# The moving operand of every weight product read by turns from two halves of its columns, and one group of seven products fewer in eight

## The chip, the cores and the metric

The kernel runs on one core of a Trainium2 chip. The metric is the time on the device in microseconds (us), the median over runs. The engines have their usual names: TensorE (PE in the profile; its weight loads are PEld), VectorE (DVE), ScalarE (ACT), GpSimd (POOL) and SyncE (SP, which here only issues DMAs).

## What is computed

One layer of a decoder in float32, 256 tokens, model width 2048: a SwiGLU feed-forward, a mixer of two kinds of attention, a second feed-forward. The weight products are nearly all of the work.

```python
h = x + 0.5 * swiglu(rms_norm(x, g1), w_gate1, w_up1, w_down1)      # 2048 -> 5632 -> 2048
u = rms_norm(h, gm)
proj = u @ w_in        # q, k, v and forget logits of 16 forgetting heads; q, k, v of 16 + 4 + 4 windowed heads
o = concat(rms_norm(forgetting_attention), rms_norm(sliding_window_sink_attention))
h = h + o @ w_out
y = h + 0.5 * swiglu(rms_norm(h, g2), w_gate2, w_up2, w_down2)
# swiglu(x, wg, wu, wd) = (silu(x @ wg) * (x @ wu)) @ wd
```

## The kernel before

**A product.** Each float32 weight and each activation is split into a high part, rounded to the matmul's input format (fp32r), and a low part, the rest. `mm3` multiplies a 128x128 stationary block of activations with 512 columns of weights (the moving operand) as three matmuls: high by high, high by low, low by high. The three stand on lines 400, 401 and 402, whoever calls `mm3`. In the mixer one projection has blocks of 388 columns. Only these products take weights; transposes, scores and the sums over values are plain fp32 matmuls on other lines (602 turns a feed-forward's rows, 1320 makes scores).

**Making the parts.** SyncE loads a weight tile (`raw`, 128x2048 in a feed-forward), ScalarE casts it (`whi`), VectorE subtracts (`wlo`, line 464). One of four subtractions in most down parts is on GpSimd (line 466, `BESIDE`).

**Groups.** A tile of a feed-forward's up part holds four blocks of 512 columns: two rows of blocks (k) of the gate's weights and two of the up weights. With two tiles of tokens that is a 2x2 by 2x2 product of blocks. A group of kind D does it with the plain eight products. A group of kind S does it with seven, in Winograd's form: four of the seven take sums of weight blocks, which VectorE makes (line 531 the outer two, line 538 the inner two), ScalarE casts and VectorE splits again (line 464, `sums`). Sums of activations (`fu`) are made once for each pair of k (`form_of`), and VectorE combines the results at the end of a unit (line 733).

**Units.** A feed-forward goes over 11 blocks of 512 hidden columns. A unit ("U") is one block: eight groups, whose kinds the table `UNITS` gives; a down part ("D") takes the block's result through the down weights in four groups of kind D. `PLAN` has units and down parts by turns. In between stand transposes (line 602).

**What sets the order.** For each feed-forward `arrange` plays the tasks through with costs and due times that the code gives (a product 0.681, `cast`, `sub`, `slow` for GpSimd's subtraction) and limited buffers, and the order that comes out of it is each engine's order in the program. TensorE's own order of products is that of `main`, with the transposes put in between. In the mixer the order comes from the framework's scheduler.

Of the kernel before, what the change touches and what calls it, by code (L numbers as in the profile page):

```python
# [18 lines left out]
D = 2048  # L19
# [11 lines left out]
SWC = NSW // 4  # L31
# [3 lines left out]
    mybir.EngineType.PE, mybir.EngineType.DVE, mybir.EngineType.Activation, mybir.EngineType.Pool, mybir.EngineType.SP  # L35
}
NB = FF // 512
UNITS = [["D" * 8, x, "DSSSSSSD"] + ["SSSSSSSD"] * (NB - 3) for x in ("DDSSDSSD", "DSSDSSSD")]
DOWN = "DDDD"
BESIDE = (1,)  # L40
AT_Q2 = True
# [1 line left out]
PLAN = [("U", 0)] + [x for b in range(1, NB) for x in (("U", b), ("D", (b - 1,)))][:-1] + [("D", (NB - 2, NB - 1))]  # L43
NRAW = 4
NSUM = 2
NHI = 5
NLO = 5
SCRATCH = 512
FREE2 = 2
F2_ORDER = [(0, "rawy", F32)] + [(2, "whiy", F32R), (3, "wloy", F32R)] * FREE2 + [(1, "sums", F32)] * NSUM  # L50
F2_ORDER += [(2, "whiy", F32R)] * (NHI - 2 - FREE2) + [(3, "wloy", F32R)] * (NLO - 2 - FREE2) + [(0, "rawy", F32)] * (NRAW - 3)
PAD = 48
# [47 lines left out]


def slow(n):
    return 0.4 + 0.0021 * n


class Task:
# [167 lines left out]
def hybrid_layer(ctx: ExitStack, tc: tile.TileContext, a: dict, out: bass.AP):  # L274
# [69 lines left out]
    def mean_rsqrt(pool, ssq, n, width, tag):  # L344

        own = "rm" if pool is sp else tag
        x = pool.tile([P, n], F32, tag=own + "x", name=tag + "x")
        y = pool.tile([P, n], F32, tag=tag + "y", name=tag + "y")
        t = pool.tile([P, n], F32, tag=own + "t", name=tag + "t")
        nc.vector.tensor_scalar(  # L350
            out=x, in0=ssq, scalar1=1.0 / width, scalar2=EPS, op0=ALU.mult, op1=ALU.add
        )
        nc.vector.tensor_scalar(
            out=t.bitcast(I32), in0=x.bitcast(I32), scalar1=1, scalar2=None,
            op0=ALU.logical_shift_right,
        )
        nc.vector.tensor_scalar(
            out=y.bitcast(I32), in0=t.bitcast(I32), scalar1=-1.0, scalar2=float(0x5F3759DF),
            op0=ALU.mult, op1=ALU.add,
        )  # L360
        for _ in range(3):
            nc.vector.tensor_tensor(out=t, in0=y, in1=y, op=ALU.mult)
            nc.vector.scalar_tensor_tensor(
                out=t, in0=t, scalar=-0.5, in1=x, op0=ALU.mult, op1=ALU.mult
            )
            nc.vector.scalar_tensor_tensor(
                out=y, in0=t, scalar=1.5, in1=y, op0=ALU.add, op1=ALU.mult
            )
        return y
# [18 lines left out]
    def rstd_tokens(ssq, width, tag):  # L388
# [7 lines left out]
                )  # L396
        return mean_rsqrt(sp, pb[:, :NT], NT, width, tag)

    def mm3(o, shi, slo, mhi, mlo, start, stop, seeded=False):
        nc.tensor.matmul(o, lhsT=shi, rhs=mhi, start=start, stop=False, skip_group_check=seeded)  # L400
        nc.tensor.matmul(o, lhsT=shi, rhs=mlo, start=False, stop=False, skip_group_check=seeded)  # L401
        return nc.tensor.matmul(o, lhsT=slo, rhs=mhi, start=False, stop=stop, skip_group_check=seeded)  # L402
# [29 lines left out]
    def ffn(pool, u, wgu, wd, slots, banks, rstd, held=None, first=None, lead=None, done=None, out=None):  # L432
# [10 lines left out]
        def task(*args, **kw):  # L443
            t = Task(*args, **kw)
            tasks.append(t)
            return t
# [12 lines left out]
        def bank_of(b):  # L459
            return banks[b["first"].got["bank"][0]]  # L460
# [84 lines left out]

        def product(held, key, stat, w, need):

            t = task("pe", 0.681, None, list(need) + w[0], lag=0.25)
            b = held.setdefault(key, {"first": t})
            if "seed" in b and "last" not in b:  # L550
                t.need.append(b["first"])
            if b["first"] is t:
                t.take = {"bank": 1}
            b["last"] = t

            def run():
                t.made = mm3(bank_of(b), *stat(), *w[1](), start=b["first"] is t, stop=b["last"] is t, seeded="seed" in b)

            t.run = run
            main.append(t)  # L560
            return t
# [89 lines left out]
        forms = {}  # L651
        units = UNITS[0 if first is not None else 1]
        count, seven_of = [k.count("S") for k in units], PAIRS[0 if first is not None else 1]
# [195 lines left out]
                        later.append(c)  # L849

        if lead is not None:
            proj = task("pe", 10.8, None, give=[(k, list(ids)) for k, ids in held.items() if k != "bank"])
            main.append(proj)
            res = [task("dve", 0.75, lambda t=t: lead["residual"](t), [proj], 12, give=[("bank", [t])], psum=True) for t in range(NT)]
            un, ssq, gcol = lead["next"]
            lead_squares = squares_of(ssq, 3, [[r] for r in res], 50)
            turned(lambda: h[:, :, 3 * 512 :], 3, res, into_u(un, gcol, 45))
# [44 lines left out]
    def more_slots(pool):  # L902

        return [
            [pool.tile([P, 2048], dt, name="%s%d" % (nm, i)) for i in range(n)]
            for nm, dt, n in (("rawx", F32, NRAW - 2), ("sums", F32, NSUM), ("whix", F32R, NHI - 2), ("wlox", F32R, NLO - 2))
        ]

    def join(slots, own_first):

        raws, sums, his, los = slots
        return [
            (x + r if own_first else r + x) for r, x in ((rings[0], raws), ([], sums), (rings[1], his), (rings[2], los))
        ]
# [66 lines left out]
    with tc.tile_pool(name="mix", bufs=1) as mp:  # L981
# [197 lines left out]
        for t in range(NT):  # L1179
            for aa in range(2):  # L1180
                n = nqk // 2
# [211 lines left out]
    with tc.tile_pool(name="f2", bufs=1, reuse_waits=REUSE) as fp:  # L1393
        slots = [[], [], [], []]
        for i, nm, dt in F2_ORDER:
# [3 lines left out]
            fp, u2, a["wgu2"], a["wd2"], join(slots, True), acc, lambda: rstd_blocks(ss2, "rm"),  # L1399
            {"hi": range(FREE2, NHI), "lo": range(FREE2, NLO), "bank": (0, 1)},  # L1400
            lead={"residual": last_quarter, "next": (u2, ss2, V_G2)}, out=out.rearrange("(t p) d -> p t d", p=P),
# [4 lines left out]
def _arrays(x, positions, norm_ffn1_g, ffn1_w_gate, ffn1_w_up, ffn1_w_down, norm_mix_g, w_in, b_forget,  # L1406
            fox_q_norm_g, fox_k_norm_g, swa_q_norm_g, swa_k_norm_g, swa_sinks, out_norm_fox_g, out_norm_swa_g,
            w_out, norm_ffn2_g, ffn2_w_gate, ffn2_w_up, ffn2_w_down):
    f32 = np.float32
    d = {}  # L1410

    def blocks(w, rows, cols):

        n, m = w.shape
        w = w.reshape(n // P // rows, rows, P, m // cols, cols).transpose(3, 0, 2, 1, 4)
        return w.reshape(m // cols, n // P // rows, P, rows * cols)

    def cols(w):
        return blocks(w, 2, 512)

    def twos(w0, w1):

        x = np.stack([cols(w0).reshape(-1, w0.shape[0] // (2 * P), P, 2, 512), cols(w1).reshape(-1, w1.shape[0] // (2 * P), P, 2, 512)])
        x = np.stack([x[0, ..., 0, :], x[0, ..., 1, :], x[1, ..., 1, :], x[1, ..., 0, :]], -2)
        return x.reshape(*x.shape[:-2], 2048)

    def by_two(w):
        v = w.reshape(w.shape[0], -1, 2, 512)
        return twos(v[:, :, 0].reshape(w.shape[0], -1), v[:, :, 1].reshape(w.shape[0], -1))

    d["wgu1"], d["wd1"] = twos(ffn1_w_gate[0], ffn1_w_up[0]), by_two(ffn1_w_down[0])
    d["wgu2"], d["wd2"] = twos(ffn2_w_gate[0], ffn2_w_up[0]), by_two(ffn2_w_down[0])
    w = w_in[0]
    nf = NH * HD
    d["ws"] = blocks(w[:, 3 * nf :], 2, SWC)
    d["wf"] = np.stack([blocks(w[:, i * nf : (i + 1) * nf], 2, 512) for i in range(3)], 1)
    d["wo"] = np.stack([cols(w_out[0][:nf]), cols(w_out[0][nf:])])
    d["xT"] = x[0].T.reshape(KD // 2, 2, P, SEQ).transpose(0, 2, 1, 3)
    d["x"] = x[0].reshape(NT, P, D)
    d["pos"] = positions[0].reshape(NT, P).T  # L1440

    vec = np.zeros((P, V_END), f32)
    for col, g in (
        (V_G1, norm_ffn1_g), (V_GM, norm_mix_g), (V_G2, norm_ffn2_g), (V_GF, out_norm_fox_g), (V_GS, out_norm_swa_g),
    ):
        n = g.shape[1] // P
        vec[:, col : col + n] = g[0].reshape(n, P).T
    vec[:, V_BF : V_BF + NH] = b_forget[0]
    vec[:, V_SINK : V_SINK + NH] = swa_sinks[0]
    vec[:, V_SQ : V_SQ + HD] = swa_q_norm_g[0]  # L1450
    vec[:, V_SK : V_SK + HD] = swa_k_norm_g[0]
    vec[:HD, V_FQ] = fox_q_norm_g[0]
    vec[:HD, V_FK] = fox_k_norm_g[0]
    vec[HD : HD + 2, V_FQ : V_FK + 1] = 1.0
    d["vec"] = vec

    cst = np.zeros((P, C_END), f32)
    i, j = np.arange(P)[:, None], np.arange(P)[None, :]
    cst[:, C_ID : C_ID + P] = i == j
    cst[:, C_ONE : C_ONE + P] = 1.0  # L1460
    cst[:, C_TRI : C_TRI + P] = i <= j
    cst[:, C_MSK : C_MSK + P] = np.where(j > i, 0.0, NEG)
    for m in (C_MSK + P, C_MSK + 3 * P):
        cst[:, m : m + P] = np.where(j <= i, 0.0, NEG)
    cst[:, C_INVF : C_INVF + 32] = (10000.0 ** (-np.arange(0, HD, 2, dtype=np.float64) / HD)).astype(f32)
    d["cst"] = cst
    return {k: np.ascontiguousarray(v) for k, v in d.items()}
# [17 lines left out]
```

## Time and profile before

| what | value |
|---|---|
| median of 3 runs | 1734.43 us (1733.5 to 1734.45) |
| the profiled execution's own time | 1734.49 us |
| its span, first to last instruction | 1732.7 us |
| TensorE busy, matmuls | 1721.5 us (99%), 7989 |
| VectorE busy | 1557.7 us (90%) |
| ScalarE busy | 1161.1 us (67%) |
| GpSimd busy | 106.7 us (6%) |
| moved by DMA | 339.73 MB, mean 196 GB/s |

The stages lie so in the span: first feed-forward to about 650 us, mixer to about 1050 us, second feed-forward to the end. A matmul's busy time is modelled (its end is not recorded), and matmuls overlap each other; how fast TensorE goes is therefore read from the distance of starts. "wlo<-raw,whi" means that the instruction writes `wlo` and reads `raw` and `whi`. An "x8" behind a row of the timeline says that eight instructions were merged in it. A row of waits ends in total us, times and longest.

### The profile page before, as it was taken

Reading aid. Unit: us, or ns where it says so; the run is one execution under the profiler, and the core shown is the slowest. Engines: PE = TensorE matmul, PEld = TensorE weight load, DVE = VectorE, ACT = ScalarE, POOL = GpSimd, SP = SyncE. Lnnn points to the kernel's source line nnn. Section 1 sums busy time; section 2 is a strip of 40 time slices with the busy share of each in tenths; the row PEclk is TensorE's granted clock in tenths of the full one; section 3 lists DMA queues with packets and bytes.
Section 4 is the critical chain, followed back from the end, with each engine's and each line's share of the span. In section 5 each row is a group of like instructions: output and inputs, shape, how many; then the busy total and the mean of one; then the engine's idle time right before and its main releaser. Section 6 shows DMA issues by size and latency. Waiting matters only on the chain.

```text
span 1732.7 us, 21114 instructions
## 1 busy us (share of the span) xinstructions
PE 1721.5 (99%) x7989; PEld 1431.7 (83%) x7989; DVE 1557.7 (90%) x1724; ACT 1161.1 (67%) x1416; POOL 106.7 (6%) x40
## 2 busy tenths in 40 slices
PE   9999999999999999999999999999999999999999
PEld 6888888888888888998788888888888888888887
DVE  7999999999999996668777769999999999999994
ACT  6677777767776764555766556667767777776761
POOL 0011001101101100000000000001101101100100
PEclk9999999999999999999999999999999999999999
DMA  9556456556645653574444456446556646655652
GB/s 366 196 215 219 168 202 240 204 182 216 223 172 217 219 205 128 168 212 153 137 145 145 134 202 259 166 174 224 196 189 218 242 160 223 220 186 194 232 194 97
DMA packets 62918, 339.73 MB, mean 196 GB/s; under 512 B 6752, under 2 KB 15456, under 8 KB 29280
## 3 DMA queue, kind: packets, MB, share of 16 engines
q1 hardware_dynamic: 62208, 337.18, 54.8%
q8 instruction: 62, 1.02, 0.2%
q0 software_dynamic: 320, 1.05, 0.1%
q14 instruction: 40, 0.33, 0.1%
q10 hardware_dynamic: 288, 0.16, 0.0%
HBM read 336.27 MB, written 2.10 MB: 195 GB/s over the span
## 4 chain that ended last, share of the span: by engine, by line
PE 97%; DVE 1%; DMA 1%; ACT 1%; SPq 0%; issue 0%; DVEq 0%; ACTq 0%
PE acc L401 25%; PE acc L400 25%; PE acc L402 25%; PE sm L401 6%; PE sm L402 6%; PE sm L400 6%; PE acc L602 1%; PE sm L1131 1%; PE sc L1320 1%; DMA rawx<-in_wgu 1%; PE sm L1137 1%; PE sm L602 0%; PE sm L1299 0%; DVE wloy L464 0%; PE sc L1245 0%; PE sm L1138 0%
## 5 line engine op out<-in xcount | busy, mean ns | idle before, releaser
L400 PE MATMUL acc<-whi,u 128*128 128x512 f32 (+1 forms) x659 | 251.5, 383 | 1.1 <-DVE s L1095 0.9
L401 PE MATMUL acc<-wlo,u 128*128 128x512 f32 (+1 forms) x659 | 251.2, 382 | 0.8 <-DVE wlo L464 0.8
L402 PE MATMUL acc<-whi,u 128*128 128x512 f32 (+1 forms) x659 | 249.9, 381 | 0.0
L317 DVE TENSOR_TENSOR wlo<-raw,whi 128x1024 fp32r<-128x1024 f32 (+1 forms) x112 | 128.8, 1154 | 74.0 <-ACT whi L316 73.5
L316 ACT CAST whi<-raw 128x1024 fp32r<-128x1024 f32 (+1 forms) x112 | 111.0, 991 | 96.3 <-PE acc L402 87.0
L400 PEld LDWEIGHTS acc<-whi,u 128*128 128x128 f32 x659 | 123.7, 188 | 23.5 <-DVE s L1095 1.3
L401 PEld LDWEIGHTS acc<-wlo,u 128*128 128x128 f32 x659 | 123.7, 188 | 21.7 <-DVE wlo L464 1.1
L402 PEld LDWEIGHTS acc<-whi,u 128*128 128x128 f32 x659 | 123.6, 188 | 21.1 <-issue 0.8
L464 DVE TENSOR_TENSOR wlo<-sums,whi 128x2048 fp32r<-128x2048 f32 x53 | 121.2, 2287 | 3.2 <-ACT whi L519 2.3
L464 DVE TENSOR_TENSOR wlo<-raw,whi 128x1536 fp32r<-128x1536 f32 (+3 forms) x57 | 107.3, 1884 | 8.1 <-ACT whi L490 7.1
L830 ACT COPY h<-acc 128x512 f32<-128x512 f32 (+1 forms) x115 | 64.5, 567 | 69.3 <-PE acc L402 69.1
L464 DVE TENSOR_TENSOR wloy<-sums,whiy 128x2048 fp32r<-128x2048 f32 x41 | 93.7, 2286 | 2.4 <-ACT whiy L519 1.7
L464 DVE TENSOR_TENSOR wlox<-rawx,whix 128x2048 fp32r<-128x2048 f32 (+1 forms) x42 | 86.4, 2058 | 6.2 <-ACT whix L490 5.1
L464 DVE TENSOR_TENSOR wlox<-sums,whix 128x2048 fp32r<-128x2048 f32 x39 | 89.2, 2286 | 0.7
L538 DVE TENSOR_TENSOR sums<-sums,raw 128x512 f32<-128x512 f32 x130 | 87.8, 687 | 1.3
L400 PE MATMUL acc<-whi,hT 128*128 128x512 f32 x216 | 84.8, 392 | 0.0
L402 PE MATMUL acc<-whi,hT 128*128 128x512 f32 x216 | 84.1, 389 | 0.0
L401 PE MATMUL acc<-wlo,hT 128*128 128x512 f32 x216 | 84.1, 389 | 0.0
L464 DVE TENSOR_TENSOR wloy<-raw,whiy 128x2048 fp32r<-128x2048 f32 (+1 forms) x39 | 80.1, 2053 | 3.7 <-ACT whiy L514 1.8
L401 PE MATMUL acc<-wlox,u 128*128 128x512 f32 x205 | 79.9, 390 | 0.5 <-DVE wlox L464 0.5
L401 PE MATMUL acc<-wloy,u 128*128 128x512 f32 x205 | 80.0, 390 | 0.4 <-DVE wloy L464 0.3
L400 PE MATMUL acc<-whix,u 128*128 128x512 f32 x205 | 79.8, 390 | 0.0
(344 smaller groups left out, 4776.9 us busy)
## 6 DMA issues: line engine op xcount, KB each, us to landing
raw<-in_wgu SPq DMA_DIRECT2D x86, 1024.0 KB, 4.8
rawx<-in_wgu SPq DMA_DIRECT2D x44, 1024.0 KB, 4.9
raw<-in_wd SPq DMA_DIRECT2D x44, 1024.0 KB, 4.8
rawy<-in_wgu SPq DMA_DIRECT2D x44, 1024.0 KB, 4.8
raw<-in_wf SPq DMA_DIRECT2D x48, 512.0 KB, 3.3
rawx<-in_wd SPq DMA_DIRECT2D x22, 1024.0 KB, 4.8
rawy<-in_wd SPq DMA_DIRECT2D x22, 1024.0 KB, 4.8
raw<-in_wo SPq DMA_DIRECT2D x32, 512.0 KB, 3.3
```

Of the source, the lines that this page charges most:

```text
L316: nc.scalar.copy(hi, src)
L317: nc.vector.tensor_tensor(out=lo, in0=src, in1=hi.bitcast(F32), op=ALU.subtract)
L400: nc.tensor.matmul(o, lhsT=shi, rhs=mhi, start=start, stop=False, skip_group_check=seeded)
L401: nc.tensor.matmul(o, lhsT=shi, rhs=mlo, start=False, stop=False, skip_group_check=seeded)
L402: return nc.tensor.matmul(o, lhsT=slo, rhs=mhi, start=False, stop=stop, skip_group_check=seeded)
L464: tt(out=o_, in0=a, in1=f32(b), op=ALU.subtract)
L538: tt(out=s[n + 2], in0=s[2 * n], in1=cols_of(raw())[r], op=ALU.add)
L602: nc.tensor.transpose(bt[:, j * SEQ + t * P : j * SEQ + (t + 1) * P], src()[:, t, m], ident)
L830: nc.scalar.copy(o_, src)
L1131: nc.tensor.transpose(bt[:, j * P : (j + 1) * P], src[:, j, :], ident)
L1137: nc.tensor.matmul(bo[rows, c0 : c0 + SEQ], lhsT=vals(0, j), rhs=p0[:, j, :], start=True, stop=False)
L1320: nc.tensor.matmul(o_, lhsT=qk_[:, 0, j, blk * P : (blk + 1) * P], rhs=qk_[:, 1, j, 0:nk], start=True, stop=True)
```

## The change

It has three parts. First, the columns of every weight block are laid out anew by the host: the even columns first, then the odd ones (`turned`, within each block of 512 or 388 columns). `by_turns` gives the matmul a view of that block which takes a column of the first half, then one of the second, and so on, so that the products come out in the old order of columns. Casts, subtractions, sums and DMAs run over the tiles as before. Second, in nine of the eleven units of each feed-forward six groups of kind S and two of kind D stand where seven S and one D stood. Third, two of the costs by which `arrange` plays its tasks are other numbers.

```diff
-UNITS = [["D" * 8, x, "DSSSSSSD"] + ["SSSSSSSD"] * (NB - 3) for x in ("DDSSDSSD", "DSSDSSSD")]
+UNITS = [["D" * 8, x, "DSSDSSSD"] + ["SSSSSDSD"] * (NB - 3) for x in ("DDSSDSSD", "DSSDSSSD")]
...
+MM3 = 0.648
...
 def slow(n):
-    return 0.4 + 0.0021 * n
+    return 0.3 + 0.0025 * n
...
+    def by_turns(x):
+        return x.rearrange("p (x a) -> p a x", x=2)
+
     def mm3(o, shi, slo, mhi, mlo, start, stop, seeded=False):
+        mhi, mlo = by_turns(mhi), by_turns(mlo)
         nc.tensor.matmul(o, lhsT=shi, rhs=mhi, start=start, stop=False, skip_group_check=seeded)
...
-            t = task("pe", 0.681, None, list(need) + w[0], lag=0.25)
+            t = task("pe", MM3, None, list(need) + w[0], lag=0.25)
...
-            proj = task("pe", 10.8, None, give=[(k, list(ids)) for k, ids in held.items() if k != "bank"])
+            proj = task("pe", 16 * MM3, None, give=[(k, list(ids)) for k, ids in held.items() if k != "bank"])
...
+    def turned(w, n):
+        return np.swapaxes(w.reshape(*w.shape[:-1], w.shape[-1] // n, n // 2, 2), -1, -2).reshape(w.shape)
+
     def cols(w):
-        return blocks(w, 2, 512)
+        return blocks(turned(w, 512), 2, 512)
...
-    d["ws"] = blocks(w[:, 3 * nf :], 2, SWC)
-    d["wf"] = np.stack([blocks(w[:, i * nf : (i + 1) * nf], 2, 512) for i in range(3)], 1)
+    d["ws"] = blocks(turned(w[:, 3 * nf :], SWC), 2, SWC)
+    d["wf"] = np.stack([cols(w[:, i * nf : (i + 1) * nf]) for i in range(3)], 1)
```

On VectorE, the end of a unit in the first feed-forward, before the change (`raw0`, `raw1`, `rawx0` and `rawx1` are the loaded tiles, `sums0` and `sums1` the sums; a line 464 of 1536 columns belongs to a group of seven, as does one that reads `sums`; one of 2048 columns that reads a `raw` is a group of eight):

```order
L538 TENSOR_TENSOR sums1_90<-sums1_90,raw1_71 128x512
L531 TENSOR_TENSOR sums0_89<-rawx0_87 128x1024
L464 TENSOR_TENSOR wlox1_95<-raw1_71,whix1_92 128x1536
L464 TENSOR_TENSOR wlox2_96<-sums1_90,whix2_93 128x2048
L538 TENSOR_TENSOR sums0_89<-sums0_89,rawx0_87 128x512 x2
L464 TENSOR_TENSOR wlo0_74<-rawx0_87,whi0_72 128x1536
L464 TENSOR_TENSOR wlo1_75<-sums0_89,whi1_73 128x2048
L464 TENSOR_TENSOR wlox0_94<-rawx1_88,whix0_91 128x2048
L464 TENSOR_TENSOR wlox1_95<-raw0_70,whix1_92 128x2048
```

The end of a unit on VectorE after the change (lines moved down by five: 469 is 464 of before, 543 is 538):

```order
L469 TENSOR_TENSOR wlo1_75<-raw0_70,whi1_73 128x1536
L543 TENSOR_TENSOR sums0_89<-sums0_89,rawx0_87 128x512
L469 TENSOR_TENSOR wlox0_94<-sums1_90,whix0_91 128x2048
L469 TENSOR_TENSOR wlox1_95<-raw1_71,whix1_92 128x2048
L469 TENSOR_TENSOR wlox2_96<-rawx0_87,whix2_93 128x1536
L469 TENSOR_TENSOR wlo0_74<-sums0_89,whi0_72 128x2048
L469 TENSOR_TENSOR wlo1_75<-rawx1_88,whi1_73 128x2048
L469 TENSOR_TENSOR wlox0_94<-raw0_70,whix0_91 128x2048
```

In both the last two rows are the unit's last group of eight and the first of the down part. After the change one more group of eight (`raw1` into `wlox1`) stands ahead of the last group of seven, with one subtraction and no sums; over the whole program there are 115 groups of seven where there were 133.

On TensorE, the end of a unit before the change: the last three products of its last group of seven (`fu6` holds a sum of activations), then the first of the group of eight:

```order
L400 MATMUL acc_115<-whix2_93,fu6_1292 128x512
L401 MATMUL acc_115<-wlox2_96,fu6_1292 128x512
L402 MATMUL acc_115<-whix2_93,fu6_1292 128x512
L400 MATMUL acc_117<-whix2_93,u1_83 128x512
L401 MATMUL acc_117<-wlox2_96,u1_83 128x512
L402 MATMUL acc_117<-whix2_93,u1_83 128x512
L400 MATMUL acc_118<-whi0_72,u1_83 128x512
L401 MATMUL acc_118<-wlo0_74,u1_83 128x512
L402 MATMUL acc_118<-whi0_72,u1_83 128x512
```

After the change, in the same part: the end of the group of eight that is new, then the first products of the group of seven behind it (405 to 407 are 400 to 402 of before):

```order
L405 MATMUL acc_119<-whix2_93,u1_83 128x512
L406 MATMUL acc_119<-wlox2_96,u1_83 128x512
L407 MATMUL acc_119<-whix2_93,u1_83 128x512
L405 MATMUL acc_116<-whi0_72,u1_83 128x512
L406 MATMUL acc_116<-wlo0_74,u1_83 128x512
L407 MATMUL acc_116<-whi0_72,u1_83 128x512
L405 MATMUL acc_115<-whi0_72,u1_83 128x512
L406 MATMUL acc_115<-wlo0_74,u1_83 128x512
L407 MATMUL acc_115<-whi0_72,u1_83 128x512
L405 MATMUL acc_118<-whi0_72,fu5_1283 128x512
L406 MATMUL acc_118<-wlo0_74,fu5_1283 128x512
L407 MATMUL acc_118<-whi0_72,fu5_1283 128x512
```

The three matmuls of a product stand as before; in the middle of a feed-forward there are now 90 products between one set of transposes and the corresponding next, where there were 89. In the mixer each engine's instructions stand in the same order as before. SyncE's rows are the same.

## The prediction

> **What bounds the kernel now.** I read the busy table and the slices first, then the chain that ended last, then TensorE's waits, then stretches of the span side by side, and last single instructions in order of time. The page:
>
> ```profile
> span 1732.7 us, 21114 instructions
> PE 1721.5 (99%) x7989; PEld 1431.7 (83%) x7989; DVE 1557.7 (90%) x1724; ACT 1161.1 (67%) x1416; POOL 106.7 (6%) x40
> PE   9999999999999999999999999999999999999999
> DVE  7999999999999996668777769999999999999994
> PEclk9999999999999999999999999999999999999999
> ...
> PE 97%; DVE 1%; DMA 1%; ACT 1%; SPq 0%; issue 0%; DVEq 0%; ACTq 0%
> ```
>
> TensorE is busy in every slice at full granted clock, and 97% of the chain is TensorE. VectorE is nearly as full in both feed-forward stages, slack in the mixer (slices 16 to 23). Does TensorE wait for anybody? The two longest waits, and four stretches (columns: time, TensorE, weight loads, VectorE, ScalarE, GpSimd, each with its count; clock, DMA share, GB/s):
>
> ```profile
> PE sm L926 <- ACT zero L923: 2.7, 1, 2.7
> PE sm L1299 <- ACT aug L1304: 0.9, 1, 0.9
> ```
>
> ```profile
> 0.00:50.00 50.00, 45.81 (x190) 35.24 (x191) 39.29 (x77) 36.78 (x58) 0.20 (x4) 1.00 0.92 350
> 50.00:100.00 50.00, 50.00 (x226) 41.50 (x225) 47.33 (x40) 34.33 (x34) 4.63 (x1) 1.00 0.60 218
> 850.00:900.00 50.00, 48.65 (x277) 39.70 (x276) 36.38 (x70) 32.99 (x67) 3.38 (x6) 1.00 0.40 133
> 1300.00:1400.00 100.00, 100.00 (x451) 82.98 (x450) 98.81 (x86) 72.82 (x81) 10.41 (x2) 1.00 0.61 220
> ```
>
> The longest wait is the start-up. So the time is a count of matmuls times their pace. But in 1300:1400 VectorE is at 98.81 of 100 us: it would stop a faster TensorE at once if its own work stayed.
>
> A matmul's busy time here (0.39 us) is a modelled length; the pace is the distance of starts. For the 128x512 products, from a stretch that holds nothing else (first and last row, and the count of the window around them):
>
> ```profile
> 351.95 0.39 PE L400 MATMUL acc<-whi,hT 128*128 128x512 f32 x1
> ...
> 398.88 0.39 PE L400 MATMUL acc<-whix,u 128*128 128x512 f32 x1
> ```
>
> ```profile
> 352.00:398.99 46.99, 46.99 (x209) 1.00 0.49 172
> ```
>
> Of the 209, one began ahead of the first row shown: 207 steps in 46.93 us, 226.7 ns each. For the 388-wide products of the mixer, nine matmuls in a row, eight steps:
>
> ```profile
> 700.78 0.34 PE L402 MATMUL acc<-whi,u 128*128 128x388 f32 x1
> 700.96 0.33 PE L400 MATMUL acc<-whi,u 128*128 128x388 f32 x1
> 701.13 0.34 PE L401 MATMUL acc<-wlo,u 128*128 128x388 f32 x1
> ...
> 702.02 0.33 PE L400 MATMUL acc<-whi,u 128*128 128x388 f32 x1
> 702.19 0.34 PE L401 MATMUL acc<-wlo,u 128*128 128x388 f32 x1
> ```
>
> 1.41 us over eight is 176.3 ns, in steps of about 0.17 and 0.18 by turns. And two kinds of plain fp32 matmul, 256 and 128 columns wide, back to back:
>
> ```profile
> 952.81 1.89 PE L1320 MATMUL sc<-aug 66*128 66x256 f32 x8
> ```
>
> ```profile
> L1320 PE MATMUL sc<-aug x64: 272/326/382, 874.5 to 968.7; 66*128 66x128 f32 x32, 66*128 66x256 f32 x32
> ```
>
> ```profile
> 410.44 1.03 PE L602 MATMUL acc<-cst,s 128*128 128x128 f32 x8
> ```
>
> ```profile
> 410.44 0.27 PE L602 MATMUL acc<-cst,s 128*128 128x128 f32 x1
> ```
>
> Eight of 256 columns take 1.89 us with the last one's 0.382 in it: (1.89 - 0.38) / 7 = 216 ns. Eight of 128: (1.03 - 0.27) / 7 = 109 ns. The difference is 0.84 ns a column; 256 columns of it are 215 ns, so 1 or 2 ns remain as fixed cost. The product takes a column in half that time, or less: (226.7 - 176.3) / 124 = 0.41 ns. 512 columns at 0.42 are 215 ns, yet it needs 226.7: **some 11 ns of each product are lost to something that the half-rate matmuls don't pay**, though each of them has a weight load of its own too (the page counts 7989 of both).
>
> **What that loss looks like.** At 388 columns it is 176.3 - 163 = 13 ns, no smaller than at 512. So it does not grow with the columns; it looks like a stall per instruction, and steps of 0.17 and 0.18 by turns say that it depends on how the start falls against something periodic. It shows only where columns are read at full rate. A stall in the read of the moving operand fits all three; a cost of changing weights fits the first. The order of reading, which is what the change turns, can act on the former and not on the latter.
>
> **The change part by part.** (1) *Reading by turns*, lines 400 to 402: 6951 products of 512 columns after the change and 384 of 388. No row of before shows a moving operand with a step, so the price is bounded: at best the fixed cost goes entirely, 215 ns; at worst each column needs a read of its own at the plain fp32 matmuls' rate, 0.84 ns a column, 430 ns. I take 216, the row of a matmul that gives the array the same 512 steps of work. Gain: 6951 x (226.7 - 216) = 74.4 us. For 388 columns, 388 x 0.42 + 1.5 = 164.5: 384 x 11.8 = 4.5 us. The table's new price of a product, 0.648 (three times 0.216, where the old 0.681 is three times 227), says for which pace the order is laid out; it shows nothing of the chip, and I count it as none.
>
> (2) *One group of seven fewer* in nine units of each feed-forward: 18 groups of eight products in place of seven. 18 x 3 = 54 more matmuls (2299 to 2317 on each of the three lines) x 226.7 = 12.2 us at the old pace. All on the path.
>
> (3) *What VectorE is relieved of.* Rows of before:
>
> ```profile
> L531 DVE TENSOR_TENSOR sums<-raw 128x1024 f32<-128x1024 f32 x65 | 78.6, 1219 | 0.3
> L538 DVE TENSOR_TENSOR sums<-sums,raw 128x512 f32<-128x512 f32 x130 | 87.8, 687 | 1.3
> L464 DVE TENSOR_TENSOR wlo<-raw,whi 128x1536 fp32r<-128x1536 f32 x28 | 49.1, 1752 | 0.9 <-ACT whi L514 0.9
> L464 DVE TENSOR_TENSOR wlo<-sums,whi 128x2048 fp32r<-128x2048 f32 x53 | 121.2, 2287 | 3.2 <-ACT whi L519 2.3
> L464 DVE TENSOR_TENSOR wlo<-raw,whi 128x2048 fp32r<-128x2048 f32 x23 | 53.1, 2309 | 3.1 <-ACT whi L490 3.1
> ```
>
> A group of seven costs 1.22 + 2 x 0.69 + 1.75 + 2.29 = 6.63 us of VectorE, a group of eight 2.31; 4.3 us less, 18 times: 78 us. Two of fourteen form preparations go too. Off the path, so worth nothing by itself; it is what lets (1) through. One unit and one down part repeat at the distance of the turned rows:
>
> ```profile
> 471.85 0.82 PE L602 MATMUL acc<-cst,s 128*128 128x128 f32 x6
> ```
>
> from 410.44 to 471.85, 61.41 us for 89 products and eight transposes. After: 270 matmuls x 216 + 8 x 0.109 = 59.2 us. VectorE needs 98.8% of 61.41, 60.7 us, less 4.3: 56.4, 95% of the new period. With seven groups of seven it would need 60.7 against 58.5, and VectorE would set the end; with six it has 2.8 us to spare. ScalarE (73%) loses two of three casts in those groups. The same twelve 1 MB blocks per period: 220 GB/s becomes 228, where the first stretch shows 350. SP's queue keeps its rows.
>
> (4) *The start* (190 matmuls in 50 us instead of 226, DMA share 0.92): it is fed by DMA, so I give back the gain on some 180 products, 1.9 us. (5) *GpSimd's price in the table* (`slow`: 4.7 to 5.4 us for 2048 columns) moves order only. (6) The host's new layout adds no transfer: blocks and sizes are the same.
>
> Sum: 1732.7 + 12.2 - 74.4 - 4.5 + 1.9 = 1667.9 us of span; with the 1.8 us that the profiled execution has around it (1734.49 against 1732.7), 1669.7. That execution stands 0.06 us from the median of 1734.43, so nothing is corrected.
>
> [...]
>
> **The rivals.** *Waits take some of it back* (or the loss is only partly of the read): the new order has less room than before, each weight tile is due 3% sooner, and GpSimd's subtractions stand as they were:
>
> ```profile
> L466 POOL TENSOR_TENSOR wlox<-raw,whix 128x2048 fp32r<-128x2048 f32 x6 | 32.5, 5411 | 338.4 <-PE acc L402 224.8 <-ACT acc L802 57.4 <-PE sm L402 56.2
> ```
>
> One wait of 1 to 2 us in each of 18 periods, or a pace of 219 to 222: 1688 to 1715. Against it: 2.8 us of room where 0.7 sufficed. *The pace stays*: the stall belongs to the change of weights. For it: the loss is as large at 388 columns as at 512. Then only (2) remains: 1734.5 + 12.2 = 1746.7, slower. It decides from a pace of 225 ns up, where the gain over 6951 products falls to 12 us. [...] *VectorE as bound*: shown above to need 95%; inside the first rival.
>
> **How the numbers follow.** The main case, pace 215 to 217 with waits of no weight: 66%; its own range is 1655 (less the 7 us of a 215 ns pace, and of waits in the mixer that shrink) to 1686 (1 us more in each period). The first rival 15%, the pace that stays 11%, the slower read 6%, and 2% for gains and losses that cancel within 0.2%, which is about what a measurement here tells from none. The range 1655 to 1700 holds the main case and most of the first rival. Faster 0.81, same 0.02, slower 0.17.
>
> **What the profile after would show.** Products starting 216 ns apart (2.16 us for ten), the 388-wide ones near 164 and even; TensorE still in all slices; the period of turned rows 59.2 us; VectorE some 80 us less busy in total, near 95% of a feed-forward stretch; TensorE's waits still a few us in sum. If starts stay at 227, (1) is wrong and the time is near 1747. If they are 216 but the period is over 60, look who TensorE waits for: `wlo` from VectorE or GpSimd. Most would be upset by a pace that the trace of before can't show.

## The result and the profile after

The changed kernel takes 1668.49 us (1666.33 to 1670.18), 0.9621 of the time before, 95% interval 0.9604 to 0.9637. The forecast was 1669, with 1655 to 1700 as its range. In a later session the same kernel gave 1668.39 us, ratio 0.9617 (0.9604 to 0.9630). One detail of the change as told above: in the third unit of each feed-forward it is five groups of kind S and three of kind D that stand where six and two stood; that is one group of seven fewer too, so the count of 18 holds.

> The change itself once more, for comparison on the same chip: 1668.5, ratio 0.962.

The page after, its span, busy times, two rows of slices and the chain:

```profile
span 1668.4 us, 21050 instructions
PE 1653.4 (99%) x8043; PEld 1444.8 (87%) x8043; DVE 1475.1 (88%) x1636; ACT 1127.4 (68%) x1376; POOL 98.9 (6%) x40
...
DVE  7999999999999996778777769998999999999893
...
PEclk9999999999999999999999999999999999999999
...
PE 85%; DVE 9%; issue 3%; DMA 2%; ACT 1%; SPq 0%; DVEq 0%; ACTq 0%
```

TensorE has 54 matmuls more and 64.3 us of span less. VectorE has lost 82.6 us of work. The chain now runs through VectorE for 9% of the span, which I read as TensorE and VectorE being close to balance in some places; TensorE is still busy in nearly every slice.

The pace, first and last row of a stretch of products and the count of the window around them:

```profile
402.00 0.38 PE L405 MATMUL sm<-whi,hT 128*128 128x512 f32 x1
...
448.83 0.38 PE L406 MATMUL acc<-wlox,hT 128*128 128x512 f32 x1
```

```profile
402.00:448.99 46.99, 46.99 (x219) 1.00 0.56 203
```

One of the 219 began ahead of 402.00, so there are 217 steps in 46.83 us: **215.8 ns for each matmul where it was 226.7**. The 388-wide products, which went in steps of 0.17 and 0.18 us by turns, are even now:

```profile
679.95 0.33 PE L407 MATMUL acc<-whi,u 128*128 128x388 f32 x1
680.11 0.33 PE L405 MATMUL acc<-whi,u 128*128 128x388 f32 x1
680.27 0.33 PE L406 MATMUL acc<-wlo,u 128*128 128x388 f32 x1
680.44 0.33 PE L405 MATMUL acc<-whi,u 128*128 128x388 f32 x1
```

Three steps in 0.49 us, 163 ns (176.3 before). The turned rows, one unit and one down part apart:

```profile
397.23 0.60 PE L607 MATMUL acc<-cst,s 128*128 128x128 f32 x4
...
456.39 0.60 PE L607 MATMUL acc<-cst,s 128*128 128x128 f32 x4
```

The period is 59.16 us (61.41 before). And that period as a window (columns as before: TensorE, weight loads, VectorE, ScalarE, GpSimd):

```profile
338.10:397.20 59.10, 59.10 (x279) 51.70 (x278) 56.20 (x48) 42.85 (x46) 4.58 (x1) 1.00 0.58 214
```

VectorE is busy for 56.20 of 59.10 us, 95%, where the stretch of before had 98.8%. TensorE's longest waits after the start-up are small and new in part:

```profile
PE acc L607 <- ACT h L835: 2.3, 2, 1.3
PE acc L405 <- DVE s L1100: 0.9, 1, 0.9
PE acc L406 <- DVE wlox L469: 0.8, 1, 0.8
```

### The profile page after: what moved, and what is told of

It reads as the page before. It is cut to its first block, busy times and chain, and to the rows that moved or that the text cites. A ratio compares the mean times of both kernels' runs of the same rounds, so it can differ in the third digit from the quotient of the medians.

```text
span 1668.4 us, 21050 instructions
## 1 busy us (share of the span) xinstructions
PE 1653.4 (99%) x8043; PEld 1444.8 (87%) x8043; DVE 1475.1 (88%) x1636; ACT 1127.4 (68%) x1376; POOL 98.9 (6%) x40
## 4 chain that ended last, share of the span: by engine, by line
PE 85%; DVE 9%; issue 3%; DMA 2%; ACT 1%; SPq 0%; DVEq 0%; ACTq 0%
PE acc L406 22%; PE acc L405 22%; PE acc L407 22%; PE sm L406 5%; PE sm L407 5%; PE sm L405 5%; DVE wlo L469 2%; DVE sums L536 2%; DVE wlox L469 2%; DVE wloy L469 1%; DVE sums L543 1%; DMA raw<-in_wd 1%; PE acc L607 1%; PE sm L1136 1%; PE sc L1325 1%
## 5 line engine op out<-in xcount | busy, mean ns | idle before, releaser
L405 PE MATMUL acc<-whi,u 128*128 128x512 f32 (+1 forms) x668 | 248.3, 373 | 0.9 <-DVE s L1100 0.9
L406 PE MATMUL acc<-wlo,u 128*128 128x512 f32 (+1 forms) x668 | 247.8, 371 | 0.8 <-DVE wlo L469 0.8
L407 PE MATMUL acc<-whi,u 128*128 128x512 f32 (+1 forms) x668 | 246.6, 371 | 0.0
L405 PEld LDWEIGHTS acc<-whi,u 128*128 128x128 f32 x668 | 126.4, 189 | 17.2 <-DVE s L1100 1.3
L407 PEld LDWEIGHTS acc<-whi,u 128*128 128x128 f32 x668 | 126.2, 189 | 14.8 <-issue 0.8
L469 DVE TENSOR_TENSOR wlo<-raw,whi 128x2048 fp32r<-128x2048 f32 (+3 forms) x58 | 110.8, 1912 | 9.4 <-ACT whi L495 9.3
L469 DVE TENSOR_TENSOR wlo<-sums,whi 128x2048 fp32r<-128x2048 f32 x46 | 105.3, 2289 | 4.5 <-ACT whi L524 4.5
L406 PE MATMUL acc<-wlox,u 128*128 128x512 f32 x244 | 92.7, 380 | 0.8 <-DVE wlox L469 0.8
L405 PE MATMUL acc<-whix,u 128*128 128x512 f32 x244 | 92.6, 379 | 0.0
L407 PE MATMUL acc<-whix,u 128*128 128x512 f32 x244 | 92.5, 379 | 0.0
L406 PE MATMUL acc<-wloy,u 128*128 128x512 f32 x227 | 86.1, 379 | 0.4 <-DVE wloy L469 0.4
L495 ACT CAST whi<-raw 128x2048 fp32r<-128x2048 f32 (+2 forms) x37 | 63.8, 1724 | 33.4 <-PE acc L407 15.8
L405 PE MATMUL acc<-whiy,u 128*128 128x512 f32 x227 | 86.1, 379 | 0.0
L407 PE MATMUL acc<-whiy,u 128*128 128x512 f32 x227 | 86.0, 379 | 0.0
```

What stands on the lines that cost most here:

```text
L469: tt(out=o_, in0=a, in1=f32(b), op=ALU.subtract)
L495: c.run = lambda raw=raw, hi=hi: nc.scalar.copy(hi(), raw())
```

## Experiments on the change: its parts one at a time

**The groups alone.** Contiguous reading, weights laid out as before, the new table of groups, a product's cost in the table as before:

```diff
-        mhi, mlo = by_turns(mhi), by_turns(mlo)
...
-MM3 = 0.648
+MM3 = 0.681
```

(GpSimd's cost stays the change's.)

> The new table of groups alone: contiguous reading, weights laid out as before, a product's price in the table 0.681. Theory: products start 226.7 ns apart, 54 matmuls more, 1734.3 + 12.2 = 1746.5 (1744 to 1749), TensorE without waits, VectorE about 80 us less busy. Rival (VectorE at 98.8% did cost TensorE something before): nearer 1740.

1747.15 us, ratio 1.0076 (1.0059 to 1.0093). A window of it:

```profile
300.00:400.00 100.00, 100.00 (x446) 82.71 (x445) 89.65 (x71) 69.09 (x68) 4.95 (x2) 1.00 0.57 208
```

TensorE is full, VectorE down to 89.65%, and nothing is gained by that: 13.2 us are lost against the 1733.97 us of before in the same session, the 54 matmuls at the old pace being 12.2 of them. The prediction's rival "the pace stays" had this time as 1746.7.

**Reading by turns alone.** The change with the old table of groups:

```diff
-UNITS = [["D" * 8, x, "DSSDSSSD"] + ["SSSSSDSD"] * (NB - 3) for x in ("DDSSDSSD", "DSSDSSSD")]
+UNITS = [["D" * 8, x, "DSSSSSSD"] + ["SSSSSSSD"] * (NB - 3) for x in ("DDSSDSSD", "DSSDSSSD")]
```

> Reading by turns and its costs as in the change, but the old table with seven of eight groups of seven. Theory V (VectorE is the next bound, and the eighth group makes room): products still start 216 ns apart, but VectorE needs some 60.7 us of each period against 58.5 of TensorE, so TensorE waits for wlo and sums in the middle of both feed-forwards, the period is 60.5 to 61, VectorE near 99% there, and the time is 1695 to 1712 (the mixer's 15 us and the early units are gained all the same). Rival (the groups are without effect on what waits): TensorE still bounds, 54 matmuls fewer at 216, 1668.5 - 11.7 = 1657.

1684.14 us, 0.9712 (0.9697 to 0.9726): between the two theories. One period of it (turned rows 59.83 us apart) and its longest waits but for the start-up:

```profile
345.40:405.30 59.90, 59.69 (x277) 50.92 (x276) 59.83 (x53) 44.98 (x48) 6.68 (x1) 1.00 0.59 210
```

```profile
PE acc L406 <- DVE wlox L469: 3.6, 3, 2.1
PE acc L406 <- DVE wlo L469: 2.7, 3, 1.1
```

VectorE is busy for 59.83 of 59.90 us, and TensorE, which needs only 89 x 3 x 0.2158 + 0.9 = 58.5, is held to that. So the theory of VectorE held in what bounds and missed in the amount: the period is 59.8, not 60.5 to 61, and the time 1684, not 1695 to 1712. VectorE's instructions standing back to back show why:

```profile
388.98 2.29 DVE L469 TENSOR_TENSOR wlox<-rawx,whix 128x2048 fp32r<-128x2048 f32 x1
391.18 2.29 DVE L469 TENSOR_TENSOR wlox<-raw,whix 128x2048 fp32r<-128x2048 f32 x1
```

Each lasts 2.29 us, but they start 2.20 us apart: 0.09 us of each lies beside its neighbour. Of the 50 pairs of neighbours in a period 48 overlap here, where 40 of the same 50 did in the period of before at 349 us (60.5 us busy, 0.9 us of gaps). The busy time of VectorE in a period with gaps, 60.5 us, thus overstated what it needs for the same instructions when it has none, 59.83.

**VectorE's load put back, with TensorE's work left as it is.** The change, with one more run of the same subtraction for two groups of eight in each of nine units (`arrange` is told the doubled cost, so it lays the order out anew):

```diff
-                l.run = lambda raw=raw, hi=hi, lo=lo: low(lo(), raw(), hi(), behind)
+                l.run = lambda raw=raw, hi=hi, lo=lo: [low(lo(), raw(), hi(), behind) for _ in range(2 if twice else 1)]
```

> The change, with the subtraction of two groups of eight in each of nine units of a feed-forward done twice over (same values): TensorE's work is the change's, VectorE's is that of turns_only (2 x 2.2 us more in each period). Theory V (the eighth group pays by relieving VectorE, which would otherwise bound): VectorE near 99.8%, the period about 60 instead of 59.16, waits of TensorE for wlo, 1680 to 1688. Rival (what the new table buys is the order of groups, and VectorE had room): 1668 to 1671, period 59.2.

1703.05 us, 0.9822 (0.9806 to 0.9839). One period, and the waits:

```profile
347.60:408.40 60.80, 59.38 (x279) 51.71 (x278) 60.56 (x50) 43.38 (x46) 5.73 (x1) 1.00 0.56 208
```

```profile
PE acc L406 <- DVE wlo L469: 9.2, 7, 1.7
PE acc L406 <- DVE wlox L469: 7.2, 6, 1.7
```

With the change's own groups, two more subtractions on VectorE take the period from 59.16 us to 60.84 and cost 34.6 us in all, more than expected; VectorE is busy for 60.56 of the 60.80 us. The room that the eighth group makes on VectorE is thus what the new table buys; without it, TensorE's pace can't be used in full. The loss is larger than in reading by turns alone although VectorE's durations add up to about as much in a period (64.0 and 64.5 us): fewer neighbours overlap, 41 of 48 pairs where 48 of 50 did, and the two runs of the same subtraction, which write the same tile, start 2.32 us apart and not 2.20. TensorE's wait in a period stands at a doubled subtraction, 1.4 to 1.7 us a time.

**The costs in the table.** The change with the old three costs:

```diff
-MM3 = 0.648
+MM3 = 0.681
-    return 0.3 + 0.0025 * n
+    return 0.4 + 0.0021 * n
...
-            proj = task("pe", 16 * MM3, None, give=[(k, list(ids)) for k, ids in held.items() if k != "bank"])
+            proj = task("pe", 10.8, None, give=[(k, list(ids)) for k, ids in held.items() if k != "bank"])
```

> The change with the old three costs in the table (0.681 a product, 10.8 for the projection, GpSimd's subtraction 4.7 us): the same work in an order laid out for a slower TensorE. Theory (the costs are of little weight, as VectorE has room): 1668 within 5 us. Rival (the order is what keeps TensorE from waiting): over 1675, with waits for wlo in each period.

1675.54 us, 0.9664 (0.9650 to 0.9678): some 7 us, 0.4%, are the order's, for the three costs together. The rival was right that there are waits in every period, but they aren't for `wlo`:

```profile
PE acc L607 <- DVE hT L469: 6.6, 16, 0.8
```

Sixteen times some 0.4 us, at the transposes. That the order laid out for a slower TensorE puts them where TensorE arrives too early is my reading, not tested further.

## Experiments on the seven groups: three ways that didn't pay

VectorE had 2.9 us of room in each period of the change, and a seventh group of seven saves TensorE 0.65 us. Can some of that be had?

**Seven in every second of the last eight units, or in three of four.**

```diff
-["SSSSSDSD"] * (NB - 3)
+["SSSSSDSD", "SSSSSSSD"] * ((NB - 3) // 2)
```

> The change with seven groups of seven in every second of the last eight units of each feed-forward (eight groups of seven more than the change). Theory (VectorE has room on the mean of two periods, 57.7 us of 58.8): TensorE saves 24 matmuls x 216 = 5.2 us, 1663. Rival (VectorE's peaks can't be spread over two periods, the buffers are too few): waits of 0.5 us in each period with seven, 1667 and no gain.

> Three of every four of those units with seven groups of seven. TensorE would save 36 matmuls, 7.8 us, 1660.7; VectorE needs 58.8 us a period on the mean where TensorE needs 58.7, so waits return: 1662 to 1668 by the theory that VectorE bounds there, 1660.7 by the rival that the 15.6 us lost with seven everywhere came from the early units alone.

In these two, a group of eight in a unit that follows one with seven groups of seven reads activations that the sums of activations for that pair have overwritten; instructions and sizes are those intended, so the times stand. 1684.20 us (0.9711) and 1684.76 us (0.9715). Both theories were wrong by some 20 us in each. Two periods of the first. In the upper one VectorE makes seven groups of sums and in the lower one six, while TensorE has 90 products in the upper and 89 in the lower, since VectorE works ahead:

```profile
340.10:401.50 61.40, 59.98 (x280) 51.49 (x279) 60.34 (x53) 45.34 (x49) 6.65 (x1) 1.00 0.56 203
401.50:460.10 58.60, 58.60 (x276) 51.20 (x275) 56.10 (x48) 42.19 (x45) 4.60 (x1) 1.00 0.61 218
```

VectorE has 2.5 us left over in the light period; the heavy one runs to 61.4 us, with VectorE busy for 60.34 of them; the mean is 60.0, worse than 59.16. The room of the light period is not used for the heavy one, though even that one has 1.1 us of gaps on VectorE. My reading was that seven groups in a row use up VectorE's lead, which the few tile buffers limit; the next two runs were to test it.

**The group of eight in the middle, and one down tile split without VectorE.**

```diff
-["SSSSSSSD"] * (NB - 3)
+["SSSSDSSS"] * (NB - 3)
...
-DOWN = "DDDD"
+DOWN = "DDDL"
```

(the first edit of reading by turns alone is `mid`, the second `low_dma`, both together `mid_low`)

> Reading by turns with seven of eight groups of seven as in turns_only, but the group of eight of the last eight units stands in the middle (SSSSDSSS) instead of at the end. Theory M (VectorE's mean work, 59.8 us a period as measured in turns_only, sets the end): no change, 1682 to 1685, period 59.8, VectorE over 99.5%. Rival B (the run of seven groups in a row eats up VectorE's lead, which the buffers limit): the waits go, the period falls to 58.6, 1662 to 1668.

> turns_only with one of the four down tiles of a period split without VectorE: ScalarE writes minus the high part and a DMA adds the weights to it (kind L). VectorE's mean falls by 2.2 us to 57.5 of 58.6. Theory M alone: the waits go, 1662 to 1668. Theory B (a run of sevens is longer than the lead): waits of about 1.3 us a period stay as in half_sevens, 1680 to 1684. If the adding DMA is late, TensorE waits for it in the down parts and it is slower than 1690.

> Both: the group of eight in the middle, and one down tile of a period split by ScalarE and DMA. If M and B are both at work, neither alone is enough and this one is: TensorE bounds at 58.6 a period, 54 matmuls fewer than the change, 1657 to 1662, below the change. If the adding DMA is late: slower than 1690.

1696.54 us (0.9782), 1695.96 us (0.9780) and 1694.64 us (0.9775, 0.9761 to 0.9790): all slower than with the old table alone, against both theories. For the two with the adding DMA a further case was on record, slower than 1690 if that DMA is late, and it is the one that came. The longest waits of TensorE, of the first and of the second:

```profile
PE acc L405 <- ACT acc L807: 16.0, 11, 2.5
PE sm L405 <- ACT sm L807: 6.8, 3, 3.1
```

```profile
PE acc L406 <- DMA wlo<-in_wd: 4.7, 6, 1.3
PE acc L406 <- DMA wlox<-in_wd: 4.0, 4, 1.7
```

And ScalarE in the first, ahead of the longest of those waits (it ends at 399.04):

```profile
393.88 0.59 ACT L807 COPY acc<-h 128x512 f32<-128x512 f32 x1
396.60 1.90 ACT L495 CAST whix<-rawx 128x2048 fp32r<-128x2048 f32 x1 [2.13 <-DMA rawx<-in_wd]
398.40 0.58 ACT L807 COPY sm<-h 128x512 f32<-128x512 f32 x1
```

With a group of seven at the end of a unit, the down part's first products wait for ScalarE to put the old sums into banks (line 807). The banks come free as VectorE combines the unit's results (line 738); for this copy that was at 398.07. But the copy also stands behind a cast of a down tile on ScalarE, here and in nearly all of these waits, and begins 0.2 to 1.3 us after its bank is free; that is some 10 of the 22.8 us. With the DMA that adds, the split tile is late (11.3 us of such waits in the second). So the group of eight at the end of a unit seems to cover the combination and the copies behind it (not tested by itself), and neither edit tests the theory of the lead: what limits a unit with seven beyond VectorE's own work stays open.

## Experiments on the read itself

**Matmuls alone.** The layer is left out; 32 matmuls of each kind stand back to back, each with one of eight stationary blocks in rotation. `view` is the way of reading; the weights lie as they are, not laid out anew, so only the read differs. (An excerpt of the code; one execution of each of the two kernels.)

```python
for i in range(32):
    nc.tensor.matmul(o[:m, :n], lhsT=s[:k, i % 8 * P : i % 8 * P + m], rhs=view(w[:k, i % 4 * 512 : i % 4 * 512 + n]), ...)
# turns(x, b): rearrange("p (x a b) -> p a x b")   near(a): "p (g x a) -> p g a x", x=2   step(x): "p (a x) -> p x a"
```

> A kernel of matmuls alone, 32 back to back for each way of reading the moving operand (fp32r, 128x512 unless said), each with a weight load of its own from eight blocks by turns; the layer is left out. Contiguous reading should start every 226.7 ns and two halves by turns every 216, as in the two traces. Theory W (the weight load's own reads get in the way of the contiguous read): with 64 stationary columns instead of 128 contiguous reading loses about half of the 11 ns (221), with 32 a quarter (219); 256 and 384 moving columns lose the same 11 ns (120 and 173). Theory C (a property of the contiguous read alone, so much per column): 64 or 32 stationary columns change nothing (226), and 256 columns lose half (115). On the places: if two far apart lines in turn are what helps, then four or eight places by turns (256 or 128 columns apart) do as well (216), and turns between neighbours 16 bytes apart do not (227). If any two reads in a row must only not share 16 bytes, neighbours 16 bytes apart and steps of four columns do it too (216), and pieces of 4 or 8 columns do not (227). [...] bf16 operands: 216 either way.

> Matmuls alone again, 32 back to back for each way of reading, the layer left out: contiguous and two halves by turns at 128, 256, 384, 448 and 512 columns, and other pieces. Theory F (contiguous reading pays a fixed amount per instruction, by turns does not): the difference stays 8 to 11 ns from 256 columns up, so that by turns wins 7% at 256 and 5% at 512. Theory C (an amount per column): the difference grows with the columns, 5 ns at 256 and 10 at 448. Turns between neighbours 8 bytes apart (near of two columns): 227 if each of the two streams must stay in its 16 bytes for four columns, 216 if any distance does. Near of eight: 216 by both. Plain fp32, 256 columns: 216 however it is read, if the half rate is the array's; faster by turns if it is the read's.

Rows of the timeline of the first (a row merges a block; its time contains the last matmul's own length; in order: contiguous, two halves by turns, neighbours 64 columns apart by turns, steps of four, bf16 contiguous, bf16 by turns):

```profile
11.56 7.65 PE L51 MATMUL flata<-whi,u 128*128 128x512 f32 x32
19.04 7.07 PE L51 MATMUL turns<-whi,u 128*128 128x512 f32 x32
90.93 7.07 PE L51 MATMUL near<-whi,u 128*128 128x512 f32 x32
112.02 14.93 PE L51 MATMUL step<-whi,u 128*128 128x512 f32 x32
169.49 7.08 PE L51 MATMUL bfflat<-wb,ub 128*128 128x512 bf16 x31
176.40 15.18 PE L51 MATMUL bfturns<-wb,ub 128*128 128x512 bf16 x31
```

And of the second (256 to 448 columns, contiguous and by turns; neighbours of two and of eight columns by turns):

```profile
33.37 3.94 PE L51 MATMUL flatn<-whi,u 128*128 128x256 f32 x31
37.27 3.62 PE L51 MATMUL turnsn<-whi,u 128*128 128x256 f32 x31
40.84 5.54 PE L51 MATMUL flatn<-whi,u 128*128 128x384 f32 x31
46.39 5.20 PE L51 MATMUL turnsn<-whi,u 128*128 128x384 f32 x31
51.59 6.45 PE L51 MATMUL flatn<-whi,u 128*128 128x448 f32 x31
58.08 6.03 PE L51 MATMUL turnsn<-whi,u 128*128 128x448 f32 x31
64.13 7.23 PE L51 MATMUL near<-whi,u 128*128 128x512 f32 x31
71.20 7.08 PE L51 MATMUL near<-whi,u 128*128 128x512 f32 x32
```

Start to start, from all starts of a block:

| read (fp32r, 512 columns unless said) | ns |
|---|---|
| contiguous | 227 (median) |
| two halves by turns, 256 columns apart | 215.8 |
| neighbours by turns, 64, 8 or 4 columns apart | 215.8 |
| neighbours by turns, 2 columns apart | 227 (median) |
| two halves by turns in pieces of 2, 4, 8 columns | 328, 251, 243 |
| four quarters, eight eighths by turns | 282, 489 |
| steps of 2, steps of 4 columns | 451, 461 |
| contiguous, 64 or 32 stationary columns | 230, 232 |
| 384 columns: contiguous, by turns | 173.6, 162.4 |
| 448 columns: contiguous, by turns | 202.8, 189.1 |
| 256 columns: contiguous, by turns | 122 (mean), 111.6 |
| 128 columns: contiguous, by turns | 110.0, 111.5 |
| plain fp32, 256 columns: contiguous, by turns | 216, 273 |
| bf16: contiguous, by turns | 216, 484 |

What follows. *The weight load's reads in the way* falls: with half or a quarter of the stationary columns the loss is no smaller (230 and 232 ns, where 128 columns take 227). *An amount per column* falls: 11.2 ns are lost at 384 columns, 13.7 at 448, 11 at 512 (at 256 by turns stands at the 111.5 ns of 128 columns, so I take it that another bound is reached there). The loss is nearly fixed for an instruction and belongs to contiguous reading of fp32r; bf16 read contiguously starts every 216 ns. *The places*: the distance does not matter from 4 columns (16 bytes) up, 215.8 ns at 4, 8, 64 and 256; at 2 columns by turns is as slow as contiguous (227). Just two streams, and one column at a time from each, do it: pieces of two (328 ns), or four streams (282), are slower than contiguous (227). Among the fp32r rows of 512 columns the fast ones, 215.8 ns, are just those in which every other read goes on to the neighbouring column and two reads in a row are 4 columns or more apart; bf16 and plain fp32, slower by turns (484 for 216, 273 for 216), do not follow this. Why contiguous reading loses its 11 to 14 ns per instruction stays open. Uneven steps are no sign of the loss: the contiguous 384-wide matmuls start every 173 or 174 ns and lose it all the same.

## Why the prediction was right

- *Pace.* 216 taken, 215.8 measured, and 163 to 164 for 388 columns where 164.5 was taken. The choice rested on the plain fp32 matmuls, which took 0.84 ns a column, twice the products' 0.41, and had 1 or 2 ns of fixed cost. That the missing 11 ns were the read's was an argument from three signs, and the matmuls alone show it. The sign of the uneven steps was luck: they are gone at 388, but 384 contiguous columns lose as much in even steps. And that this order of reading would end the loss was not worked out from any row of before, as the prediction itself says; the table has more orders that slow the read than ones that speed it, so that step was a bet that came out.
- *The loss as a stall per instruction* was read rightly from 388 against 512 columns, and the runs of matmuls alone show it. It had spoken for the rival that the pace stays as much as for the change; the rival's own time, 1746.7, is what the groups alone take (1747.15).
- *Groups.* 54 matmuls, and VectorE at 95% of the new period, came out as worked out: 56.2 us for 56.4. The saying that VectorE's relief is "worth nothing by itself" is shown by the groups alone, and that it lets the pace through by reading by turns alone and by the doubled subtraction.
- *Period.* 59.2 forecast, 59.16 measured; span 1667.9 forecast, 1668.4 measured. That the span is so close is partly small things that cancel: the mixer, from turned rows to turned rows, falls by 20.3 us (436.15 to 415.83) where the pace alone gives 18.7, and the last such period of each feed-forward takes 59.7 and 60.0 us where its 89 products need 58.5.
- *A term that was off:* with seven groups VectorE was put at 60.7 us of a period. It needs 59.8, since more of its instructions overlap, by 0.09 us each, when they stand back to back. That did not enter the sum.
- *A term put at nothing:* the new costs of the table. With the old ones the time is 7 us longer, so "waits of no weight" leant on them.
- *An end of the range:* 1686 is 1667.9 + 18, a span; as a time it is 1688, where the first rival begins.
- *Waits* of the first rival are there, a few us in all (2.3 us for line 835), too few to bring the time to 1688.
- *The slower read*, 6% in the forecast, did not come true for this pattern: no row of before shows a read by turns, so the 6% and a pace of 430 ns were an estimate of mine, and two halves by turns took 215.8 ns. It stands close by all the same: four streams instead of two would have been 282 ns, 66 ns more for each of 6951 matmuls, some 460 us.
- "Plain fp32 matmul" rows of the prediction: each such matmul of 256 columns stands in the trace as two instructions (64 rows, 216 ns apart, for 32 matmuls issued in the second run of matmuls alone). The 216 ns were those of one instruction, as the prediction used them.

## What to carry to other kernels

Compare start-to-start distances of a kernel's matmuls with those of other matmuls in the same trace: a fixed remainder that only some of them pay, 11 to 14 ns here, can point to how their operands are read, which a run of matmuls alone then tests. When an engine that sets the time is made faster, work out in the same stroke what the next engine needs per period; here two thirds of a microsecond of TensorE given away in each period bought 4.3 us of VectorE, and without that a quarter of the gain would have been lost. After a change of pace, give the new one to whatever lays out the order: 0.4% here, with GpSimd's cost among the three.

## What the runs showed of the hardware that I had not expected

- Reading the moving operand from two places by turns speeds an fp32r matmul of 512 columns from 227 to 215.8 ns, and slows bf16 from 216 to 484 and one instruction of plain fp32 with 256 columns from 216 to 273.
- A step of only two columns in an fp32r read costs as much as one of four: 451 and 461 ns.
- The loss of the contiguous fp32r read is nearly fixed for an instruction (11 to 14 ns from 384 to 512 columns) and not a matter of how many stationary columns are loaded (227, 230 and 232 ns with 128, 64 and 32).
- Two VectorE instructions of 2.29 us, back to back, start 2.20 us apart (with seven groups of seven, at 388.98 and 391.18 us).
